# One slab forward in a seven-product FFN chunk: order of a down slab, a later block load and an accumulator bank

## The chip, the cores and the metric

The kernel runs on one core of one Trainium2 chip, in one launch. The metric is the device time of the launch in microseconds (us).

## The reference

Two layers over 256 tokens of 1024 values (fp32). Each layer has a SwiGLU FFN, a mixer (convolution, linear recurrence and pooling side by side), a cross attention over 256 memory rows, and a second SwiGLU FFN, each with a residual and a layer norm. The change lies in the FFNs alone:

```python
def swiglu(x, w_gate, w_up, w_down):          # x 256x1024, d_ff = 2816
    return (jax.nn.silu(x @ w_gate) * (x @ w_up)) @ w_down

for l in range(2):
    h = layer_norm(ALPHA * h + 0.5 * swiglu(h, ffn1_gate[l], ffn1_up[l], ffn1_down[l]), ...)
    # mixer, cross attention
    h = layer_norm(ALPHA * h + 0.5 * swiglu(h, ffn2_gate[l], ffn2_up[l], ffn2_down[l]), ...)
```

## The kernel before

**Arithmetic.** fp32 values are kept as two parts, a high and a low one: `split` (L61, L62) has ScalarE cast the source to the high part and VectorE subtract that from the source to give the low part. A product then takes three matmuls (high x high, low x high, high x low; `mm_rows` and L112), which all accumulate in one PSUM bank. Weights come in raw tiles of 128x1024 (512 KB), and each is split into a `whi` and a `wlo` tile. These two pools have 8 buffers each, so a new split waits until TensorE is done with the part 8 back.

**An FFN.** `ffn()` goes through the hidden width in chunks of 512 columns (the last has 256). For a chunk it forms gate and up products for the 256 tokens (two halves of 128), applies SiLU and the multiplication, and `turn` brings the result to the layout that the down projection needs (four DMAs at L455, two transposes on VectorE, a split into `ah` and `al`). The down projection is cut in slabs: `both(c, u)` loads half of chunk `c`'s rows of `down`, splits it and issues 24 matmuls into four banks named `dn`, which are held open through the whole FFN. Slabs run one or two chunks behind the hidden chunks.

**The seven-product chunk.** Chunks in `sevens` don't form the eight block products (2 token halves x gate and up x 2 halves of the 1024 inputs) but seven, in the manner of Strassen, with sums of weight blocks and of blocks of x (`bx`, prepared once per FFN). There are two such chunks in the first FFN and three in each of the other three: 11 in all. The function is `by_seven`. Its four weight blocks are `w00` and `w10` (gate, upper and lower inputs) and `w01` and `w11` (up), two raw tiles each. Their homes rotate from chunk to chunk over three pairs of buffers (`spare0/1`, `lng/lnb` and two of the six `raw`).

`parts_of(r, plus)` adds a second block to the first in place on VectorE (L606), if there is one, and splits it. `run(o, x, w)` issues a product's 12 matmuls of 128x512. `taken` copies a bank to SBUF on ScalarE (L635), `put` combines a bank with SBUF on VectorE (L625), and `more` adds a block's other half of inputs to a raw tile by an accumulating DMA from GpSimd's queue (L643). Each chunk takes banks from the pool `acc`, which has 4, as `dn` has.

In program order before the change, a chunk does on TensorE:

| step | product | into | behind it |
| --- | --- | --- | --- |
| 1 | x00 x `w00` | `o[0]` | `taken` to `s` |
| 2 | bx0 x (`w00+w01`) | `o[1]` | `more(w01)` |
| 3 | x01 x `w10` | `o[2]` | |
| 4 | bx1 x (`w00+w01+w11`) | `o[0]`, added | `more(w00)`, `put(s)`, `taken(e)` |
| 5 | first slab, `between[0]` = `both(c-2, 1)` | `dn` | SiLU of `s` |
| 6 | bx2 x `w01` (with the accumulated half) | `o[0]`, added | `taken(f)` |
| 7 | second slab, `between[1]` = `both(c-1, 0)` | `dn` | `put(f)` from `o[1]` |
| 8 | bx3 x `w11` | `o[1]`, added | |
| 9 | x11 x `w00` (with the accumulated half) | `o[0]`, added | `left()`: SiLU, `put(e)` from `o[1]`, mult, `turn` |

The sum of `w11` onto `w00+w01` in step 4 is called the second sum below.

**What sets the order.** The kernel is written in program order, and a scheduler then orders the instructions of each engine by its own costs. It need not keep the order above: in the kernel before, it put matmuls of the first slab ahead of or among those of step 4 in some chunks. Each engine then runs its queue strictly in order, as do the DMA queues of SP (all loads and `turn`'s four DMAs) and of GpSimd (`more`).

Of the kernel before, what the change touches and what calls it, by code (L numbers as in the profile page):

```python
# [12 lines left out]
ALU = mybir.AluOpType  # L13
# [4 lines left out]
P = 128  # L18
# [10 lines left out]
CHUNK = 512  # L29
# [17 lines left out]
def model(ctx: ExitStack, tc: tile.TileContext, t: dict, out: bass.AP):  # L47
# [6 lines left out]
    def acc(shape=(P, 2, SEQ), tag="acc"):  # L54
        return ps.tile(list(shape), F32, tag=tag, name=tag)
# [4 lines left out]
    def split(hi, lo, src):  # L60
        nc.scalar.copy(hi, src)  # L61
        lows.append(nc.vector.tensor_tensor(lo, src, hi.bitcast(F32), op=ALU.subtract))  # L62
# [73 lines left out]
    def mm_rows(o, xh, xl, wh, wl, start, stop, more=False):  # L136
        product(o, xh, wh, start, False, more)
        product(o, xh, wl, False, False, more)
        product(o, xl, wh, False, stop, more)

    def tok(i):
        return slice(i * P, (i + 1) * P)
# [264 lines left out]
    def ffn(l, name, n, pend=None, last=False, early=None):  # L407
        gate, up, down = (t[f"{name}_{x}"][l] for x in ("gate", "up", "down"))
        with tc.tile_pool(name="ffn", bufs=2, reuse_waits="tile") as fp:
# [19 lines left out]
            def activations():  # L429
                return fp.tile([P, NT, CHUNK], F32, tag="sg", name="sg", bufs=1)  # L430
# [3 lines left out]
            def ordered(v):  # L434
                return v.rearrange("p (a k j) -> p a k j", a=4, j=32)

            def in_order(o):
                return o.rearrange("p (a j k) -> p a k j", a=4, j=32)

            def activate(s, i, og):  # L440
                nc.scalar.activation(ordered(s[:, i, :]), in_order(og), AF.Silu)
# [9 lines left out]
            def turn(s):  # L451
                ah, al = act_tiles()
                x = fp.tile([P, 4, NT, P], F32, tag="dealt", name="dealt", bufs=1)
                for a in range(4):
                    nc.sync.dma_start(x[a * 32 : a * 32 + 32], s[:, :, a * P : (a + 1) * P])  # L455
                d = fp.tile([P, NT, 4, P], F32, tag="up", name="square", bufs=1)
                for i in range(NT):
                    nc.vector.transpose(  # L458
                        d[:, i].rearrange("p k (b r) -> p b k r", b=4),
                        x[:, :, i, :].rearrange("p b (k j) -> p b k j", k=4),  # L460
                    )
                d = d.rearrange("p i k t -> p k i t")
                split(*(y.rearrange("p k (i t) -> p k i t", i=NT) for y in (ah, al)), d)
                return ah, al
# [110 lines left out]
            def by_seven(c0, bx, between):  # L575
                def rows_by_columns(r):
                    return r.rearrange("p (k c) -> p k c", c=CHUNK)

                def pieces(*tags):
                    return [  # L580
                        rows_by_columns(
                            (fp if "spare" in g else wp).tile([P, DM], F32, tag=g, name="raw", bufs=6 if g == "raw" else 1)
                        )
                        for g in tags
                    ]

                def block(m, j, to):
                    for i in range(2):
                        k = 4 * j + 2 * i
                        loads.append(nc.sync.dma_start(  # L590
                            to[i], m[k * P : (k + 2) * P, c0 : c0 + CHUNK].rearrange("(k p) c -> p k c", p=P)
                        ))
                    return to

                homes = [("spare0", "spare1"), ("lng", "lnb"), ("raw", "raw")]
                n = sevens.index(c0 // CHUNK)
                w00 = block(gate, 0, pieces(*homes[n % 3]))
                w01 = block(up, 0, pieces(*homes[(n + 1) % 3]))
                w10 = block(gate, 1, pieces("spare2", "raw"))
                w11 = block(up, 1, pieces(*homes[(n + 2) % 3]))  # L600

                def parts_of(r, plus=None):
                    hi, lo = [], []
                    for i in range(2):
                        if plus is not None:
                            nc.vector.tensor_tensor(r[i], r[i], plus[i], op=ALU.add)  # L606
                        h = wp.tile([P, 1024], F32R, tag="whi", name="whi", bufs=8)
                        w = wp.tile([P, 1024], F32R, tag="wlo", name="wlo", bufs=8)
                        h, w = (rows_by_columns(x) for x in (h, w))
                        split(h, w, r[i])  # L610
                        hi.append(h)
                        lo.append(w)
                    return Weights(hi, lo, 2, [])

                def part_of_x(i, j):
                    d = slice(4 * j, 4 * j + 4)
                    return xTh[:, d, tok(i)], xTl[:, d, tok(i)]

                def run(o, x, w, more=False):
                    for k in range(4):  # L620
                        wh, wl = w.at(k, slice(0, CHUNK))
                        mm_rows(o, x[0][:, k, :], x[1][:, k, :], wh, wl, k == 0 and not more, k == 3, more)

                def put(o, a, op, b):
                    nc.vector.tensor_tensor(ordered(o), in_order(a), ordered(b), op=op)  # L625

                s = activations()  # L630
                ef = fp.tile([P, NT, CHUNK], F32, tag="up", name="halves", bufs=1)
                e, f = ef[:, 0, :], ef[:, 1, :]

                def taken(o, bank):
                    nc.scalar.copy(ordered(o), in_order(bank))  # L635

                o = [acc((P, CHUNK)) for _ in range(3)]
                run(o[0], part_of_x(0, 0), parts_of(w00))
                taken(s[:, 0, :], o[0])
                def more(to, m, j):  # L640
                    for i in range(2):
                        k = 4 * j + 2 * i
                        nc.gpsimd.dma_start(  # L643
                            to[i], m[k * P : (k + 2) * P, c0 : c0 + CHUNK].rearrange("(k p) c -> p k c", p=P),
                            accum_op=ALU.add,
                        )

                run(o[1], bx[0], parts_of(w00, w01))
                more(w01, up, 1)
                run(o[2], part_of_x(0, 1), parts_of(w10))  # L650
                run(o[0], bx[1], parts_of(w00, w11), True)
                more(w00, gate, 1)
                put(s[:, 0, :], o[2], ALU.add, s[:, 0, :])
                taken(e, o[0])
                between[0]()
                nc.scalar.activation(s[:, 0, :], s[:, 0, :], AF.Silu)
                run(o[0], bx[2], parts_of(w01), True)
                taken(f, o[0])
                between[1]()
                put(f, o[1], ALU.subtract, f)  # L660
                run(o[1], bx[3], parts_of(w11), True)
                run(o[0], part_of_x(1, 1), parts_of(w00), True)


                def left():
                    activate(s, 1, o[0])
                    put(e, o[1], ALU.subtract, e)
                    nc.vector.tensor_tensor(s, s, ef, op=ALU.mult)  # L668
                    return turn(s)

                return left
# [27 lines left out]
            bx = []  # L699
# [541 lines left out]
```

## Time and profile before

| what | before |
| --- | --- |
| three timed runs | 1079.6, 1079.92 and 1082.12 us; median 1079.92 us |
| profiled execution | 1078.62 us, of it 1076.9 us span |
| mean granted TensorE clock | 0.999 |
| bytes read from HBM | 239.22 MB, 223 GB/s over the span |
| instructions | 16377 |

In the views that follow, PE is TensorE's matmuls and PEld its weight loads, DVE is VectorE, ACT ScalarE, POOL GpSimd and SP the engine that issues the loads. A row of a timeline has a start, a duration (both in us), the engine, the line of the kernel, the operation with `out<-in`, the shapes, a count of instructions that were put together, and in brackets how long the engine sat idle before it and whose work ended that. A row of the waits has the waiting engine and tile, what it waited for, then the total in us, the number of times and the longest. In a chain's row stand the start, the length and the work. Matmuls are pipelined, so a matmul's own duration (0.38 us) is longer than the distance between two starts.

The seven-product chunks lie at about 76 to 136 us (first FFN), 420 to 512 us, 589 to 681 us and 949 to 1041 us.

### The profile page before, as it was taken

The numbers are of one execution on the slowest core, as the hardware profiler recorded it, in microseconds if no ns is written. First come the engines' busy times: TensorE is split into PE (matmuls) and PEld (weight loads), VectorE is DVE, ScalarE is ACT, GpSimd is POOL, SyncE is SP. The second block draws the span as 40 slices with busy tenths as digits, with TensorE's granted clock in tenths as the row PEclk, the third lists the DMA queues.
The fourth block names the chain that finished last, engine by engine and source line by source line (L and its number), as shares of the span: only waits on it lengthen the run. The fifth ranks groups of instructions, "written<-read, shape, count | busy, mean of one in ns | idle before, by whom it ended". The sixth has DMA issues, their size and how long they took to land.

```text
span 1076.9 us, 16377 instructions
## 1 busy us (share of the span) xinstructions
PE 1056.5 (98%) x5918; PEld 925.8 (86%) x5918; DVE 947.1 (88%) x1257; ACT 671.2 (62%) x920; POOL 119.0 (11%) x158
## 2 busy tenths in 40 slices
PE   9999999999999999999999999999999999999997
PEld 7888788989889888888888888888898998888886
DVE  6979987998998799999798999888989788999986
ACT  7548665757467566668475767566764665666661
POOL 9701101000000001110001011010000000001100
PEclk9999999999999999999999999999999999999999
DMA  9999993764475589999679999857536665899981
GB/s 366 263 296 252 252 324 133 251 196 161 173 263 174 179 269 255 285 270 289 225 269 260 278 300 225 315 175 230 189 128 213 240 228 177 274 286 259 225 283 41
DMA packets 142864, 254.98 MB, mean 237 GB/s; under 512 B 10112, under 2 KB 49312, under 8 KB 142784
## 3 DMA queue, kind: packets, MB, share of 16 engines
q1 hardware_dynamic: 129024, 228.49, 63.2%
q0 software_dynamic: 13184, 24.27, 13.2%
q10 hardware_dynamic: 576, 1.18, 0.3%
q8 instruction: 46, 0.75, 0.3%
q14 instruction: 34, 0.28, 0.1%
HBM read 239.22 MB, written 1.05 MB: 223 GB/s over the span
## 4 chain that ended last, share of the span: by engine, by line
PE 69%; DVE 14%; DMA 6%; issue 6%; ACT 5%; SPq 1%; DVEq 0%; ACTq 0%
PE acc L112 47%; PE dn L112 20%; DVE wlo L62 6%; ACT whi L61 4%; DMA dealt<-sg 2%; DVE raw L606 2%; DMA raw<-in_ffn_gate_dram 1%; DMA raw<-in_ffn_up_dram 1%; PE acc L179 1%; SPq L455 1%; DVE square L458 1%; DMA raw<-in_ffn_down_dram 1%; DVE sg L668 1%; PE dn L943 1%; ACT ah L61 0%
## 5 line engine op out<-in xcount | busy, mean ns | idle before, releaser
L61 ACT CAST whi<-raw 128x1024 fp32r<-128x1024 f32 (+1 forms) x462 | 465.8, 1041 | 202.2 <-PE dn L112 58.9
L62 DVE TENSOR_TENSOR wlo<-raw,whi 128x1024 fp32r<-128x1024 f32 (+1 forms) x462 | 544.0, 1208 | 51.1 <-ACT whi L61 42.4
L112 PE MATMUL acc<-whi,xT 128*128 128x512 f32 x872 | 266.5, 380 | 0.0
L112 PEld LDWEIGHTS acc<-whi,xT 128*128 128x128 f32 x872 | 164.8, 189 | 23.3
L112 PE MATMUL acc<-wlo,xT 128*128 128x512 f32 x436 | 165.2, 379 | 0.0
L112 PE MATMUL acc<-xT,whi 128*128 128x512 f32 x576 | 142.2, 382 | 0.4 <-DVE xT L62 0.3
L112 PE MATMUL dn<-wlo,ah 128*128 128x512 f32 x346 | 132.2, 382 | 2.6 <-DVE wlo L62 2.6
L112 PE MATMUL dn<-whi,ah 128*128 128x512 f32 x346 | 129.9, 382 | 4.5 <-ACT whi L61 3.3
L112 PE MATMUL dn<-whi,al 128*128 128x512 f32 x346 | 130.3, 380 | 0.3
L112 PEld LDWEIGHTS acc<-xT,whi 128*128 128x128 f32 x576 | 103.9, 190 | 12.7 <-ACT whi L61 0.9
L112 PEld LDWEIGHTS acc<-wlo,xT 128*128 128x128 f32 x436 | 82.4, 189 | 11.5
L112 PE MATMUL dn<-whi,xT 128*128 128x512 f32 x288 | 87.9, 381 | 0.0
L112 PEld LDWEIGHTS dn<-whi,ah 128*128 128x128 f32 x346 | 65.2, 189 | 16.4 <-ACT whi L61 4.9
L112 PEld LDWEIGHTS acc<-xT,wlo 128*128 128x128 f32 x576 | 75.5, 191 | 3.9
L112 PEld LDWEIGHTS dn<-wlo,ah 128*128 128x128 f32 x346 | 65.4, 189 | 14.8 <-DVE wlo L62 6.0
L112 PE MATMUL acc<-xT,wlo 128*128 128x256 f32 x576 | 75.9, 275 | 0.0
L112 PEld LDWEIGHTS dn<-whi,al 128*128 128x128 f32 x346 | 65.1, 189 | 11.3 <-DVE al L62 2.3
L112 PE MATMUL acc<-whi,kTh 128*128 128x512 f32 x176 | 67.5, 384 | 3.4 <-ACT halves L635 1.8
L112 PE MATMUL acc<-wlo,kTh 128*128 128x512 f32 x176 | 66.7, 379 | 0.0
L112 PE MATMUL acc<-whi,kTl 128*128 128x512 f32 x176 | 66.7, 379 | 0.0
L357 POOL TENSOR_TENSOR rs<-rs,nhalf 128x1 f32<-128x1 f32 x16 | 14.9, 933 | 434.0 <-DVE rs L353 307.1
L112 PEld LDWEIGHTS dn<-whi,xT 128*128 128x128 f32 x288 | 54.4, 189 | 7.7 <-DVE xT L62 0.3
(236 smaller groups left out, 1357.8 us busy)
## 6 DMA issues: line engine op xcount, KB each, us to landing
raw<-in_ffn_up_dram SPq DMA_DIRECT2D x88, 512.0 KB, 5.7
raw<-in_ffn_down_dram SPq DMA_DIRECT2D x88, 512.0 KB, 6.4
raw<-in_ffn_gate_dram SPq DMA_DIRECT2D x84, 512.0 KB, 5.9
raw<-in_w_in_dram SPq DMA_DIRECT2D x48, 512.0 KB, 4.8
raw<-in_ffn_up_dram POOLq DMA_DIRECT2D x22, 512.0 KB, 6.0
raw<-in_ffn_gate_dram POOLq DMA_DIRECT2D x22, 512.0 KB, 7.9
dealt<-sg SPq DMA_DIRECT2D x80, 128.0 KB, 4.3
raw<-in_ca_k_dram SPq DMA_DIRECT2D x16, 512.0 KB, 5.1
```

Of the source, the lines that this page charges most:

```text
L61: nc.scalar.copy(hi, src)
L62: lows.append(nc.vector.tensor_tensor(lo, src, hi.bitcast(F32), op=ALU.subtract))
L112: nc.tensor.matmul(o, w, x, start=start, stop=stop, skip_group_check=more)
L179: nc.tensor.transpose(pt[:, k, :], src[:, (4 * j + k) * P : (4 * j + k + 1) * P], unit)
L357: nc.gpsimd.tensor_tensor(rs, rs, nhalf[:, 0:1], op=ALU.pow)
L455: nc.sync.dma_start(x[a * 32 : a * 32 + 32], s[:, :, a * P : (a + 1) * P])
L458: nc.vector.transpose(d[:, i].rearrange("p k (b r) -> p b k r", b=4), x[:, :, i, :].rearrange("p b (k j) -> p b k j", k=4),)
L606: nc.vector.tensor_tensor(r[i], r[i], plus[i], op=ALU.add)
L668: nc.vector.tensor_tensor(s, s, ef, op=ALU.mult)
L943: nc.tensor.matmul(o[g, hh, :], kc[:, hh, g], x, start=True, stop=True)
```

## The change

In a seven-product chunk the first slab moves from behind step 4 to in front of it, and `put(s)` with it. `w11` is loaded after that slab (program order), no longer with the other three blocks. The second slab moves from behind bx2 to in front of it. bx3's product gets a fourth bank, `o[3]`, and no longer accumulates on `o[1]`. `e` is therefore formed in two steps: `o[1]` is taken early, and `o[3]` is added in `left()`, one VectorE instruction more in each chunk. Matmuls and DMAs are the same in number and size.

```diff
                 w10 = block(gate, 1, pieces("spare2", "raw"))
-                w11 = block(up, 1, pieces(*homes[(n + 2) % 3]))
...
+                o = [acc((P, CHUNK)) for _ in range(3)]
+                run(o[0], part_of_x(0, 0), parts_of(w00))
+                taken(s[:, 0, :], o[0])
                 run(o[1], bx[0], parts_of(w00, w01))
                 more(w01, up, 1)
                 run(o[2], part_of_x(0, 1), parts_of(w10))
+                between[0]()
+                put(s[:, 0, :], o[2], ALU.add, s[:, 0, :])
+                w11 = block(up, 1, pieces(*homes[(n + 2) % 3]))
                 run(o[0], bx[1], parts_of(w00, w11), True)
                 more(w00, gate, 1)
-                put(s[:, 0, :], o[2], ALU.add, s[:, 0, :])
                 taken(e, o[0])
-                between[0]()
+                between[1]()
                 nc.scalar.activation(s[:, 0, :], s[:, 0, :], AF.Silu)
+                put(e, o[1], ALU.subtract, e)
                 run(o[0], bx[2], parts_of(w01), True)
                 taken(f, o[0])
-                between[1]()
+                o.append(acc((P, CHUNK)))
+                run(o[3], bx[3], parts_of(w11))
                 put(f, o[1], ALU.subtract, f)
-                run(o[1], bx[3], parts_of(w11), True)
                 run(o[0], part_of_x(1, 1), parts_of(w00), True)
 
                 def left():
                     activate(s, 1, o[0])
-                    put(e, o[1], ALU.subtract, e)
+                    put(e, o[3], ALU.add, e)
                     nc.vector.tensor_tensor(s, s, ef, op=ALU.mult)
                     return turn(s)
```

The three lines with a plus at `o = [acc(...)` stood a little higher before, ahead of the definition of `more`; they are not new.

More of the change, by code (lines that the diff above doesn't have):

```diff
@@ L635, in taken @@
                     nc.scalar.copy(ordered(o), in_order(bank))
-                o = [acc((P, CHUNK)) for _ in range(3)]
-                run(o[0], part_of_x(0, 0), parts_of(w00))
-                taken(s[:, 0, :], o[0])
                 def more(to, m, j):
```

## Prediction

> **What bounds the kernel now.** I read the page's first two parts, then the chain of waits, then what TensorE waits for, then the timelines around the block-product chunks.
>
> ```profile
> span 1076.9 us, 16377 instructions
> PE 1056.5 (98%) x5918; PEld 925.8 (86%) x5918; DVE 947.1 (88%) x1257; ACT 671.2 (62%) x920; POOL 119.0 (11%) x158
> PEclk9999999999999999999999999999999999999999
> ```
> ```profile
> 380.76 33.67 PE acc L112 x156
> ```
>
> TensorE is busy 98% of the span at a full clock. The second fence is a piece of the chain: 156 matmuls of 128x512 in 33.67 us, 0.2158 us from start to start. The change keeps every matmul, so only time in which that beat is broken can be won. The next view lists what TensorE itself (not its weight loads) waited for, over the whole kernel.
>
> ```profile
> PE dn L112 <- ACT whi L61: 3.3, 4, 0.9
> PE dn L112 <- DVE wlo L62: 2.6, 7, 1.0
> PE acc L112 <- ACT halves L635: 1.8, 2, 1.6
> PE acc L112 <- ACT sg L635: 1.6, 4, 0.8
> ```
> ```profile
> 123.53 0.38 PE L112 MATMUL acc<-whi,xT 128*128 128x512 f32 x1
> 124.77 0.48 PE L112 MATMUL dn<-whi,ah 128*128 128x512 f32 x1 [0.87 <-ACT whi L61]
> ```
>
> These four groups are 9.3 us, and they lie in the chunks that the change touches. A gap costs more than its idle column: from 123.53 to 124.77 is 1.24 us, 1.02 over the beat, for 0.87 idle, thus 0.15 more for each of the 17. That makes about 12 us, 1.1% of the span, and it bounds any gain from above.
>
> What makes these gaps is VectorE, which has almost as much to do there as TensorE. The first row here is a window over most of a second chunk of the FFN at 420 to 530 us, with busy time of PE, PEld, DVE, ACT and POOL, clock and DMA share; the second covers the third.
>
> ```profile
> 453.00:482.00 29.00, 28.02 (x128) 23.59 (x127) 27.69 (x27) 20.97 (x24) 3.90 (x4) 1.00 1.01 269
> 482.00:512.00 30.00, 28.89 (x137) 24.59 (x136) 27.90 (x28) 22.09 (x25) 2.38 (x2) 1.00 0.94 279
> ```
>
> **A ledger of VectorE's lead.** A chunk is 7 products of 12 matmuls and two slabs of 24, 132 in all, or 132 x 0.2158 = 28.5 us of TensorE. VectorE's turn of the second chunk goes from its first split, at the end of the first row here, to the same split one chunk on.
>
> ```profile
> 434.97 3.82 DVE L62 TENSOR_TENSOR wlo<-raw,whi 128x1024 fp32r<-128x1024 f32 x3 [0.65 <-ACT whi L61]
> 453.89 6.90 DVE L62 TENSOR_TENSOR wlo<-raw,whi 128x1024 fp32r<-128x1024 f32 x6 [1.17 <-ACT whi L61]
> 469.78 1.22 DVE L62 TENSOR_TENSOR wlo<-raw,whi 128x1024 fp32r<-128x1024 f32 x1 [0.39 <-ACT whi L61]
> 470.92 0.68 DVE L625 TENSOR_TENSOR halves<-acc,halves 128x512 f32<-128x512 f32 x1
> 471.52 1.21 DVE L606 TENSOR_TENSOR raw<-raw 128x1024 f32<-128x1024 f32 x1
> ```
> ```profile
> 445.35 0.38 PE L112 MATMUL acc<-whi,xT 128*128 128x512 f32 x1
> 456.30 0.48 PE L112 MATMUL dn<-wlo,ah 128*128 128x512 f32 x1 [0.22 <-DVE wlo L62]
> 460.56 0.48 PE L112 MATMUL acc<-whi,kTh 128*128 128x512 f32 x1 [0.76 <-ACT sg L635]
> ```
>
> The third split of the first row starts at about 437.5, so the turn is 469.78 - 437.5 = 32.3 us, 3.8 more than TensorE's. TensorE begins the last product (`x11`) of the chunk before at 445.35 and the second chunk 12 matmuls later, at 447.94: VectorE is 10.4 us ahead there. A split takes 1.15 us from start to start (6.90 for six), a `put` 0.60 (470.92 to 471.52), a sum or a mult, of a split's size, 1.15 too.
>
> The lead needed is set by the first down slab. Its first low part is the second split of the row at 453.89, over at 456.2. TensorE wants it at its second slab matmul, and in this chunk the planner had put slab matmuls right behind `w10`: 447.94 + 37 x 0.2158 = 455.9. The lead needed is 10.4 plus the 0.22 us of the idle column: it is just missed. The second wait, 0.76 us, is `taken(s)` standing in ScalarE's queue behind seven casts.
>
> **The change, part by part.**
>
> *Slab ahead of the second sum.* The slab's splits now come ahead of the splits of the second sum (`w00+w11`) in VectorE's order. In the second chunk 13 of its instructions remain from the first split to the slab's first low part: 7 splits, 3 sums (the scheduler leaves one half of the second sum in front), 2 puts, 1 mult, so 11 x 1.15 + 2 x 0.60 = 13.9 us. VectorE also waits in its alternation with ScalarE, 1.2 us (the 1.17 above) to 2. TensorE takes 37 x 0.2158 = 7.98 us to that matmul. Lead needed: 7.1 to 7.9 us. In the third chunk both halves of that sum are behind, 12.7 us of work: 5.9 to 6.75, and I take 6.75, because the one ScalarE wait that shows is 1.17 and the changed order has a `put` more that can wait.
>
> *One more put a chunk.* `put(e, o[3], ADD, e)` is new: 11 of them, 0.60 us each by the start-to-start above, 0.68 by the whole row.
>
> ```profile
> L625 DVE TENSOR_TENSOR halves<-acc,halves x22: 678/682/684, 108.6 to 1035.0; 128x512 f32<-128x512 f32 x22
> who waited for it (us, times):
>   ACT whi L61: 0.5, 1
> ```
>
> VectorE's turn goes from 32.3 to 32.9, or stays at 32.4 where its wait of 1.17 shortens. If TensorE followed VectorE at every step, 11 x 0.68 = 7.5 us would be the price; with the lead as cover, nothing. The ledger below carries it.
>
> *The lead at the start of a chunk becomes smaller.* The pools of `whi` and `wlo` have 8 buffers, so the cast of the next chunk's first block half goes when TensorE is done with the part 8 back.
>
> ```profile
> 436.48 1.05 ACT L61 CAST whi<-raw 128x1024 fp32r<-128x1024 f32 x1 [0.24 <-PE acc L112]
> 452.81 6.73 ACT L61 CAST whi<-raw 128x1024 fp32r<-128x1024 f32 x7 [4.08 <-DVE raw L606]
> 459.92 0.59 ACT L635 COPY sg<-acc 128x512 f32<-128x512 f32 x1 [0.38 <-ACT whi L61]
> ```
>
> In the first row that cast is let go by TensorE at 436.48: 8 back is the first half of `bx[2]`'s block, which stands before the second slab. In the new order 8 back is the first half of the second slab, now before `bx[2]`: released 42 matmuls, 9.07 us, before the next chunk, where the release at 436.48 was 11.46 before 447.94. The lead becomes 10.4 - 2.4 = 8.0 us.
>
> *The three later FFNs.* Second chunk: a lead of 8.0 against a need of 7.1 to 7.9, no loss. Third chunk: the lead is less by a turn's deficit, 32.4 to 32.9 against 28.5, so 3.6 to 4.1, I take 4.0; needed 6.75; a gap of 2.75 and 0.15, thus 2.9 us. The wait behind the seven casts goes, since `taken(s)` stands behind fewer. Before, the waits of these three FFNs were 9.3 less the first FFN's 4.0 (below), in 12 gaps: 5.3 + 12 x 0.15 = 7.1 us. After, 3 x 2.9 = 8.7: the change costs +1.6. With the need at 5.9 and the lead at 4.1 it is 3 x 1.95 = 5.9, a gain of 1.2; with the lead at 3.6 and a miss in the second chunk of as much as its idle column before (0.22), 3 x 3.7, a loss of 4.
>
> *The first FFN* (chunks at 76 to 136 us) has only two such chunks, so no third that pays the debt.
>
> ```profile
> PE dn L112 <- DVE wlo L62: 1.0, 1, 1.0
> PE dn L112 <- ACT whi L61: 0.9, 1, 0.9
> PE acc L112 <- ACT sg L635: 0.3, 1, 0.3
> ```
> ```profile
> 122.73 1.99 ACT L61 CAST whi<-raw 128x1024 fp32r<-128x1024 f32 x2 [5.40 <-DVE raw L606]
> ```
>
> These three are TensorE's waits from 76 to 136 us beside the `halves` group above, which lies wholly here (1.6 and 0.2): 4.0 us idle. The slab's first cast stands 5.40 us behind the second sum (122.73); with the slab ahead of it the two `dn` waits go, 1.9 + 2 x 0.15 = 2.2 us. The short `sg` and `halves` waits, 0.3 + 0.2 + 2 x 0.15 = 0.8, I count as gone too, as with fewer casts in front of those copies. The long one, 1.6, is `bx[2]` waiting for `taken(e)`. In the new order that copy stands behind a cast which waits for the gate accumulate (7.8 us to land, below), so I leave it. Gain 3.0 us; 4.75 if the copy is in time, 0.6 if its wait doubles and the short ones stay.
>
> *The fourth block's load behind the slab.* SP now issues `w11`'s two loads after the slab's.
>
> ```profile
> 464.87 5.08 SPq L590 DMA_DIRECT2D raw<-in_ffn_up_dram  x4
> ```
> ```profile
> raw<-in_ffn_up_dram SPq DMA_DIRECT2D x4, 512.0 KB, 4.9
> raw<-in_ffn_down_dram SPq DMA_DIRECT2D x3, 512.0 KB, 7.8
> raw<-in_ffn_gate_dram POOLq DMA_DIRECT2D x2, 512.0 KB, 7.8
> ```
>
> These are issues and median us to landing in the second chunk. `w11` is wanted a slab later too, so I count its move at nothing. What it must not meet is the third chunk's `w01`: its home is the second chunk's `w11`, free from the first split of `bx[3]`'s block, and the sum that reads it follows six VectorE instructions later (five splits, a put): 5 x 1.15 + 0.60 = 6.35 us. Before, the issue at 464.87 and the sum at 471.52 left 6.65. At 4.9 us it is in time. [...]
>
> *A bank for `bx[3]`.* The product no longer waits until `put(f)` has read `o[1]`. But nothing waited: in the rows on L625 its only waiter is a cast, 0.5 us. Nothing is won, and nothing lost while a fourth `acc` bank is free, since the next chunk's first product takes one that was read long before. The Trainium skill (PSUM — Partial Sum Buffer, "PSUM bank collisions raise a hardware error") says that two engines must never touch one bank's quadrant together, so an own bank should take a wait off TensorE; the sum by it would be lower by that wait, which the trace does not have.
>
> **Sum.** -3.0 + 1.6 = -1.4 us. The profiled run took 1078.62 (span 1076.9 and 1.72 around it), so 1077.2 for such a run. The three timed runs have a median of 1079.92, 1.3 above; I predict 1079.92 - 1.4 = 1078.5. About 0.3%, 3.2 us, is what can be told from no change.
>
> **Rivals.**
>
> *A, all waits go.* The slab in front gives so much slack that the ring of 8 doesn't matter: -12, 1068. For it: the waits behind the second sum are the largest. Against: VectorE's turn stays over TensorE's by 4 us. Half way, -6: 1074, if the third chunk's need is met because VectorE's 1.2 to 2 us of waits shrink and `taken(e)` comes in time. Chance of over 3.2 us gained: 0.32.
>
> *B, VectorE's work shows at the end.* The put, 0.68 us, is paid in both the second and third chunk of three FFNs (4.1 us) on top of the sum: +2.7, 1082.6. For it: 27.69 us busy in a window of 29. Against it: the third chunk's gap lets VectorE catch up. It lies within the forecast's range.
>
> *C, slower: `w01` comes late.* Third chunk only, three FFNs; each us of landing over 6.35 delays VectorE's sum, and so the slab, one for one. To be slower by 3.2 it takes (3.2 + 1.4)/3 = 1.55 over, a landing of 7.9.
>
> ```profile
> 53.08 9.91 DMA dealt<-sg
> 1031.69 7.97 DMA raw<-in_ffn_down_dram
> ```
>
> Such landings exist in the chain. At 9.0, between the two, it costs 3 x 2.65 = 8: +6.6, 1086.5. Against it: two loads instead of four are issued there, and up loads took 4.9. The copy of `e` with its wait doubled and the leads at their worst (+3.4) end there too; this side gets 0.22.
>
> *D, nothing moves.* The planner orders the engines, but the new order does hold in every chunk, so only the sizes can cancel; this is inside the forecast.
>
> **How the numbers follow.** Forecast, with B and D (within 3.2 us of before) 0.46, A with its half-way form 0.32, C and what ends with it 0.22. The range leaves out the full A and the far end of C: it goes from -7.5 (1072.5), a little past half of A, to +4.6 (1084.5), a landing of about 8.35.
>
> **What would show it.** Right: no TensorE wait on `dn` at 124.8; in each later FFN waits of 2 to 3 us in front of the third chunk's first slab, and none over 0.3 in the second; casts of the next chunk released by a `dn` matmul, not `acc`; VectorE's turn 32.4 to 32.9. Wrong: DVE idle on `raw<-in_ffn_up_dram` in front of a sum (C); no wait at all in the third chunk (A); a wait on `halves` over 1.7 us at about 103 (worst case of the first FFN).

## The result and the profile after

The changed kernel takes 1077.32 us (median of 20 runs, 1075.17 to 1080.84), the kernel before 1079.7 us (median of 20 runs beside them): a ratio of 0.9982 with a 95% interval of 0.9974 to 0.9989, which is 1.2 to 2.8 us. The forecast was 1.4 us less and within 0.3% of no change. The profiled execution of the changed kernel is one of its longest runs, 1080.84 us. A second execution of the same order was therefore profiled (`a1_again` below, 1076.26 us).

The page after, its span and busy times:

```profile
span 1079.1 us, 16365 instructions
PE 1057.2 (98%) x5918; PEld 927.9 (86%) x5918; DVE 953.9 (88%) x1268; ACT 670.1 (62%) x920; POOL 118.6 (11%) x158
```

What TensorE waited for after the change (total, times, longest), to be read beside the 9.3 us of before:

```profile
PE acc L112 <- ACT halves L634: 5.5, 2, 5.2
PE acc L112 <- DVE wlo L62: 2.0, 3, 0.7
PE dn L112 <- DVE al L62: 1.8, 3, 0.6
...
PE acc L112 <- ACT sg L634: 1.3, 3, 0.4
```

The `dn` waits on `whi` and `wlo` have left the list. A single wait of 5.2 us has come in, in the first FFN; in the second execution the same row is shorter:

```profile
PE acc L112 <- ACT halves L634: 3.4, 1, 3.4
```

Four stretches of the trace say where time went. Each begins and ends at the start of the same TensorE instruction in every trace (the last one at the last matmul):

| stretch (times of before) | before | before again | changed | changed again |
| --- | --- | --- | --- | --- |
| first FFN from its first seven-product chunk, 75.05 to 177.45 | 102.40 | 101.42 | 103.45 | 101.80 |
| second FFN and norm, 414.27 to 537.52 | 123.25 | 123.26 | 123.55 | 122.23 |
| third FFN and norm, 583.30 to 706.13 | 122.83 | 123.54 | 123.20 | 122.51 |
| last FFN, 943.11 to 1069.29 | 126.18 | 126.14 | 125.70 | 125.51 |

The last FFN is the cleanest: 0.4 to 0.7 us less, and 125.5 in all five experiments below that leave the three later FFNs as changed (a2, a3, a4, b2, c2). Over those five and the two traces of the table, the three later FFNs take 371.1 us in the mean, against 372.6 in the two traces of before: 1.5 us less, where single traces of one order differ by up to 2.2. The first FFN comes out the same within its own scatter of 2 us.

### The profile page after: what moved, and what is told of

It reads as the page before. It is cut to its first block, busy times and chain, and to the rows that moved or that the text cites. A ratio compares the mean times of both kernels' runs of the same rounds, so it can differ in the third digit from the quotient of the medians.

```text
span 1079.1 us, 16365 instructions
## 1 busy us (share of the span) xinstructions
PE 1057.2 (98%) x5918; PEld 927.9 (86%) x5918; DVE 953.9 (88%) x1268; ACT 670.1 (62%) x920; POOL 118.6 (11%) x158
## 3 DMA queue, kind: packets, MB, share of 16 engines
HBM read 239.22 MB, written 1.05 MB: 223 GB/s over the span
## 4 chain that ended last, share of the span: by engine, by line
PE 69%; DVE 15%; DMA 7%; issue 5%; ACT 4%; SPq 1%; DVEq 0%; ACTq 0%
PE acc L112 47%; PE dn L112 19%; DVE wlo L62 8%; DMA raw<-in_ffn_up_dram 2%; ACT whi L61 2%; DMA raw<-in_ffn_gate_dram 2%; DMA dealt<-sg 2%; DVE raw L605 1%; PE acc L179 1%; DVE square L458 1%; DVE al L62 1%; ACT ah L61 1%; DMA raw<-in_ca_k_dram 1%; DVE halves L624 1%; DMA raw<-in_ffn_down_dram 1%
```

## The experiments

All kernels are written with one switch for each part of the change, so that parts can be undone singly; `early` is set in the first FFN alone. The diffs are shortened to what a switch does. Each ratio is to the kernel before, on the same chip.

**a1, the change once more.** No edit.

> The changed kernel once more, with its by_seven written with four switches (all on); the order on every engine is the same. The profiled run of the changed kernel had one wait of 5.15 us in front of TensorE's x11 product at 117 us (first FFN), behind the copy of f. Theory 1 (that wait hangs on when the next chunk's w00 lands, and so differs from run to run): another profile shows this wait with another length, between 0 and 6 us, the three later FFNs keep 2.4 us of waits each within 0.3, and the times spread over about 5 us with a median near 1077.3. Theory 2 (it is a fixed consequence of the new order): the wait is 5.2 us again within 0.5.

Measured: 1077.33 us, ratio 0.9984 (0.997 to 0.9998), runs from 1076.02 to 1082.43. The wait was 3.4 us, so it differs from run to run (theory 1), and the later FFNs' waits in these chunks are those of the first profile, but for one of 0.3 us. Their place is the third chunk. The first three rows are TensorE's waits there, the last two the windows of the second and third chunk (busy PE, PEld, DVE, ACT, POOL, clock, DMA share), cut at the same times as those of before:

```profile
482.53 0.48 PE L112 MATMUL acc<-wlo,xT 128*128 128x512 f32 x1 [0.67 <-DVE wlo L62]
490.79 0.48 PE L112 MATMUL acc<-whi,kTh 128*128 128x512 f32 x1 [0.44 <-ACT sg L634]
494.67 0.48 PE L112 MATMUL dn<-whi,al 128*128 128x512 f32 x1 [0.59 <-DVE al L62]
```
```profile
453.00:482.00 29.00, 28.81 (x132) 24.29 (x130) 27.78 (x28) 18.79 (x22) 4.78 (x4) 1.00 0.99 284
482.00:512.00 30.00, 28.44 (x135) 24.33 (x136) 29.06 (x29) 21.38 (x26) 2.42 (x2) 1.00 0.99 279
```

The second chunk waits for nothing; the third waits 1.70 us in three places, 2.2 over the beat. VectorE is busy 29.06 of 30 us in the second window, where it was 27.90 before.

**a2, the old order in the first FFN alone.**

```diff
-    all four parts on
+    all four parts off if early is not None else all four parts on
```

> The old order of the four steps in the first FFN, the new order in the three later FFNs. Theory 1 (all of the change in time, gain and spread, is in the first FFN; the later three cost the same in both orders, 7.5 us before and 7.7 after): about 1079.7, no different from before within 0.7 us, and a spread of 3 us or less as before had. The prediction's ledger (first FFN gains 3.0, later ones lose 1.6): 1081.3. Rival (the gain comes from the later FFNs): 1077.3.

Measured: 1078.23 us, ratio 0.9989 (0.9977 to 1.0001). That is 1.2 us less than before (-0.1 to 2.5), some two thirds of the 1.7 that a1 kept, with only the later FFNs changed. It speaks against the ledger's 1081.3, and rather against theory 1, which had no gain here; it agrees with the 1.5 us of the stretches. Its runs spread over 5.6 us, where theory 1 had 3 or less. The times alone settle neither that there is a gain (the interval reaches past 1) nor whether the first FFN adds to it: the two ratios overlap.

**a3, the second slab back behind bx2 in the first FFN.** The wait of up to 5.2 us is `x11`, into `o[0]`, waiting until the copy of `f` has been read from it. Here is ScalarE's queue in front of that copy, and SP's issue of the second chunk's `w00` (the rows of two gate loads at 103.08), in the changed kernel:

```profile
105.91 0.58 ACT L634 COPY halves<-acc 128x512 f32<-128x512 f32 x1
109.61 1.05 ACT L61 CAST whi<-raw 128x1024 fp32r<-128x1024 f32 x1 [3.12 <-DMA raw<-in_ffn_gate_dram]
112.25 1.04 ACT L61 CAST whi<-raw 128x1024 fp32r<-128x1024 f32 x1 [1.59 <-DMA raw<-in_ffn_gate_dram]
113.53 1.04 ACT L61 CAST whi<-raw 128x1024 fp32r<-128x1024 f32 x1 [0.24 <-DMA raw<-in_ffn_gate_dram]
115.92 1.04 ACT L61 CAST whi<-raw 128x1024 fp32r<-128x1024 f32 x1 [1.35 <-DVE raw L605]
116.87 0.58 ACT L634 COPY halves<-acc 128x512 f32<-128x512 f32 x1
```
```profile
103.08 1.65 SPq L590 DMA_DIRECT2D raw<-in_ffn_gate_dram  x2
```

and the same issue in the kernel before, where it goes out with a third load of the gate:

```profile
98.35 3.37 SPq L590 DMA_DIRECT2D raw<-in_ffn_gate_dram  x3
```

The copy of `e` (105.91) is in time. The copy of `f` (116.87) stands behind four casts: one waits for the accumulated half of `w00`, two for the next chunk's `w00`, which was issued 4.7 us later than before, and one for a sum on it. The load is late because its home is `w01`'s, and that is read by bx2's splits, now behind the second slab's.

```diff
+    if early is None: between[1]()
     run(o[0], bx[2], parts_of(w01), True)
     taken(f, o[0])
+    if early is not None: between[1]()
```

> As changed, but in the first FFN alone the second slab stands behind bx2 again, so that the splits of w01 for bx2, which free the home of the next chunk's w00, come before the slab's. Theory 1 (the late w00 load makes the copy of f late): w00 of the second chunk is issued some 4 us earlier (before: 98.35, changed: 103.08), the wait of up to 5.15 us at 117 goes, the time is 1074 to 1076 with the narrow spread of before. Rival (the load is late because SP's queue carries w11 later): the wait stays, time 1077 to 1078.

Measured: 1080.03 us, ratio 1.0009 (0.9997 to 1.0022). The load is issued at 97.55, as theory 1 had it, and the wait for `f` is gone. But others have come, and the time is no better, where theory 1 had 1074 to 1076:

```profile
PE acc L112 <- ACT halves L634: 3.1, 3, 1.6
PE dn L112 <- DVE al L62: 2.4, 4, 0.6
PE dn L112 <- ACT ah L61: 2.1, 4, 1.0
```

The first row is now mostly bx2 waiting for the copy of `e` (1.05 and 1.63 us in the first FFN): with the second slab gone from between bx1 and bx2, both of which go into `o[0]`, nothing covers that copy. So the run does not show what an earlier load alone would bring.

**a4, `w11` loaded with the other blocks.** The order of every engine but SP stays.

```diff
+    w11 = block(up, 1, ...)          # behind w10
...
-    w11 = block(up, 1, ...)          # behind the first slab
```

> As changed, but w11 is loaded with the other three blocks, as before the change; only SP's order differs. Theory 1: the wait in front of x11 in the first FFN stays, as its load waits for the home and not for SP; 1077.3 within 1 us. Rival (w11's late load collides with the next chunk's w00 on the DMA engines): the wait falls to under 1.5 us and the time to 1075 or less. If SP's queue is instead held up by w11's wait for its home, loads behind it are late in all FFNs: over 1079.

Measured: 1077.19 us, ratio 0.9983 (0.997 to 0.9995): the same as the change (theory 1). Where `w11`'s load stands costs nothing and brings nothing. The wait for `f` was 2.0 us in its profile, the shortest of the three, but the times don't differ.

**b1, the kernel before once more.** No edit.

> The kernel before once more, with its by_seven written with four switches (all off); the order on every engine is the same. It gives a second profile of it. Theory 1 (its waits are fixed by the order, and only the long wait of the first FFN for the copy of e, 1.56 us in the first profile, moves from run to run): the dn waits at 124 us again 0.87 and 0.96, the later FFNs again 2.4 to 3.1 us each over the beat, median 1079.8. Rival (before loses more than its one profile showed): the later FFNs lose 3.5 us or more in this one.

Measured: 1079.55 us, ratio 0.9998 (0.9986 to 1.0011), theory 1. Its trace is the column "before again": the `dn` waits of the first FFN are again 0.87 and 0.97, the wait for `e` is 0.73 instead of 1.56, and the later FFNs lose 2.9 to 3.1 us each over the beat in their three chunks (2.5 to 2.9 in the first profile). This counts every gap of over 0.12 us from start to start, less the beat; by the same count a1 loses 2.4 to 2.5, of which 2.2 in the three places of the third chunk.

**b2, the copy of `f` ahead of the next chunk's casts, first FFN.**

```diff
+    with tc.issue_after(copy_of_f.ins):      # of the chunk before
+        p00 = parts_of(w00)
```

> As changed, but in the first FFN ScalarE's copy of f is ordered ahead of the casts of the second chunk's w00 (it stood behind them, and they wait for loads that land at 109 to 113 us). Theory 1 (TensorE's wait of 2.0 to 5.2 us in front of x11 is this place in the queue): the wait on halves goes or falls under 1 us; a part comes back as a wait of the second chunk's first product for its own casts, 0 to 2 us; 1074 to 1076.5. Rival (the loads are late for everything, so the wait only moves): 1077 to 1078 with waits of the same sum on whi or wlo in the second chunk's first product.

Measured: 1081.55 us, ratio 1.0013 (1.0001 to 1.0025). The rival was right that the wait only moves, and the time is even longer than it said. TensorE's waits in the first FFN are now these:

```profile
118.80 0.48 PE L112 MATMUL acc<-whi,xT 128*128 128x512 f32 x1 [1.17 <-ACT whi L61]
130.19 0.48 PE L112 MATMUL acc<-wlo,kTh 128*128 128x512 f32 x1 [0.76 <-DVE wlo L62]
146.40 0.48 PE L112 MATMUL acc<-whi,xT 128*128 128x512 f32 x1 [3.04 <-ACT halves L634]
```

The last is the same wait one chunk later: the second chunk's copy of `f` behind four casts, of which the first waited 4.09 us for a transfer of the gate.

```profile
141.99 3.88 ACT L61 CAST whi<-raw 128x1024 fp32r<-128x1024 f32 x4 [4.09 <-DMA raw<-in_ffn_gate_dram]
145.78 0.57 ACT L634 COPY halves<-acc 128x512 f32<-128x512 f32 x1
```

**b3, the first slab alone.** Of the change only `between[0]` and `put(s)` in front of the second sum.

```diff
+    between[0]()
+    put(s[:, 0, :], o[2], ALU.add, s[:, 0, :])
     run(o[0], bx[1], parts_of(w00, w11), True)
...
-    between[0]()
     run(o[0], bx[2], parts_of(w01), True)
```

> Of the change only the first slab (with put(s)) in front of the second sum; the second slab, w11's load and bx3's bank as before. The prediction's ledger: the lead at the start of a chunk stays 10.4 us as 8 parts back is again bx2's block, while the need falls to 7.9 and 6.75, so the later FFNs' waits (7.1 to 7.5 us) and the dn waits of the first FFN (2.2) nearly all go: 1070.5 to 1073. Rival (the lead is set by more than the ring, so the third chunk still waits 2 us or more): 1076 to 1078. If the copy of e becomes late in more chunks: 1079 or over.

Measured: 1093.59 us, ratio 1.0125 (1.0105 to 1.0144). The ledger's 1070.5 to 1073 is far off; it is the expectation's last case, the copy of `e` late in more chunks. Waits of TensorE, the row for the copies, and one of its eight places with ScalarE's queue there:

```profile
PE acc L112 <- ACT halves L634: 17.1, 8, 4.0
```
```profile
475.14 0.80 PE L112 MATMUL acc<-whi,kTh 128*128 128x512 f32 x1 [2.55 <-ACT halves L634]
```
```profile
473.55 1.04 ACT L61 CAST whi<-raw 128x1024 fp32r<-128x1024 f32 x1 [3.09 <-DMA raw<-in_ffn_gate_dram]
474.50 0.58 ACT L634 COPY halves<-acc 128x512 f32<-128x512 f32 x1
```

It is a3's finding on a larger scale: the slab that moves forward was the cover of the copy of `e` between bx1 and bx2, and the casts in front of the copy wait for loads. In the full change the second slab takes its place.

**b4, the bank alone.** Of the change only `o[3]` and the put that it adds.

```diff
-    run(o[1], bx[3], parts_of(w11), True)
+    o.append(acc((P, CHUNK)))
+    run(o[3], bx[3], parts_of(w11))
...
-    put(e, o[1], ALU.subtract, e)
+    put(e, o[3], ALU.add, e)                 # o[1] taken earlier by a put of its own
```

> Of the change only bx3's own bank, with the put that it adds in each chunk; the order of steps is as before. The prediction's step (nothing waited for that bank, and the put is covered by the lead or costs its 0.6 us in a chunk that waits): 1079.8 to 1082, waits of the later FFNs longer by 0 to 1.2 us each. Rival (the bank frees a wait): under 1079.

Measured: 1079.43 us, ratio 1.0002 (0.9992 to 1.0011), between the two expectations. In the old order the bank and its 11 puts together change nothing; the run does not part the two.

**c1, everything but the bank.** The reverse of b4's diff, in the new order.

> As changed, but bx3 accumulates on o[1] as before, after put(f) has read it. Theory 1 (the bank is free of worth in the old order, where the second slab stood between the copy of f and bx3, but in the new order bx2 and bx3 touch): TensorE waits at bx3 for the copy of f and put(f), 0.58 + 0.68 and their hand-overs, up to 2 us in each of 11 chunks, less what the scheduler fills with the next chunk's products: 1083 to 1095. The prediction's step (nothing is won by that bank): within 1 us of the changed kernel, 1077 to 1078.

Measured: 1095.8 us, ratio 1.0149 (1.0136 to 1.0162), theory 1. The way is not quite as expected: the scheduler filled the place with the next chunk's products, so little waits on `put(f)` itself, and the loss shows at other copies:

```profile
PE acc L112 <- ACT sg L634: 9.5, 7, 1.6
PE acc L112 <- ACT halves L634: 4.8, 8, 1.0
PE acc L112 <- ACT whi L61: 2.9, 1, 2.9
PE acc L112 <- DVE halves L624: 1.9, 5, 0.5
```

**c2, less to load in the first FFN.** The accumulate of the gate block is left out in its two chunks, so that `w00` keeps only its sum there.

```diff
-    more(w00, gate, 1)
+    if early is None: more(w00, gate, 1)
```

> As changed, but the first FFN's two chunks leave out the accumulate of the gate block's other half (4 transfers of 512 KB on GpSimd's queue), so w00 keeps only its sum there; all other instructions and their order are the same. Theory 1 (the first FFN's wait for the copy of f is set by when loads land, and the DMA engines are full there): the wait of 2.0 to 5.2 us falls under 1 us, w00's loads land 1.5 us or more earlier, 1073.5 to 1075.5. Rival (the wait is the queue's order alone): the wait stays over 2 us, 1077 to 1078.

Measured: 1074.48 us, ratio 0.9953 (0.994 to 0.9966), theory 1. The median landing time of SP's gate loads from 90 to 115 us, first in the changed kernel and then here (6.4 us in the kernel before):

```profile
raw<-in_ffn_gate_dram SPq DMA_DIRECT2D x3, 512.0 KB, 9.1
```
```profile
raw<-in_ffn_gate_dram SPq DMA_DIRECT2D x3, 512.0 KB, 4.8
```
```profile
PE dn L112 <- DVE al L62: 0.6, 1, 0.6
```

The last row, of the kernel with less to load, is all that TensorE waits for from 75 to 140 us. The first FFN's stretch takes 99.8 us and the runs lie within 1.3 us. The edit also takes away one cast's wait for the accumulate itself, so it shows that the transfers set this wait, not how much each of them does.

**c3, 7 buffers of `whi` and `wlo`.** `bufs=8` becomes `bufs=7` in both places of both pools.

> As changed, with 7 buffers of whi and of wlo instead of 8. The prediction's step on the lead (it is set by the part 8 back): with 7 the release comes 12 slab matmuls, 2.6 us, later, so the second chunk waits 2 us where it waited none and the third 2 to 4.6 us more; over three FFNs 12 to 20 us: 1089 to 1097. Rival (the lead is set by VectorE's own work or by the loads): under 1081.

Measured: 1080.99 us, ratio 1.0012 (1.0001 to 1.0022), so the rival, if only just, and far from the 1089 to 1097 of the step on the lead. TensorE's waits on low parts come more often, most of them short:

```profile
PE acc L112 <- DVE wlo L62: 6.8, 15, 1.8
```

The three later FFNs take 370.3 us in this trace, as in a1 (370.3): there a ring of 7 costs no time, though the waits stand in other places. What 7 cost lies in the rest of the kernel: outside the four stretches it takes 605.9 us of the span, against 602.2 to 604.1 in the other traces.

**c4, one put less.** `put(e, o[1], ...)` is left out, so bx0's product is missing from `e`; VectorE has 11 instructions less.

> As changed, but put(e, o[1]) is left out (the product with bx0 is missing from e); VectorE has 11 instructions less, ScalarE's, SP's and GpSimd's order is the same. The prediction's ledger (each put in the second and third chunk of a later FFN takes 0.6 us from the lead that the third chunk lacks): the third chunk's waits fall from 2.0 us idle to about 0.8 in each of three FFNs, 1073 to 1074.5. Rival (those waits stand on the ring and on turn's split of al, not on the put): 1076.5 to 1078.

Measured: 1076.49 us, ratio 0.9969 (0.9959 to 0.9979). The third chunk's waits in the second FFN, to be read beside a1's 0.67, 0.44 and 0.59:

```profile
483.56 0.48 PE L112 MATMUL acc<-wlo,xT 128*128 128x512 f32 x1 [0.25 <-DVE wlo L62]
491.82 0.48 PE L112 MATMUL acc<-whi,kTh 128*128 128x512 f32 x1 [0.44 <-ACT sg L634]
495.70 0.48 PE L112 MATMUL dn<-whi,al 128*128 128x512 f32 x1 [0.59 <-DVE al L62]
```

Only the first gives way, by 0.42 us here (0.45 and 0.20 in the next two FFNs): mostly the rival. The put costs the later FFNs about 1 us in all.

None of these, with the whole computation in it, is clearly faster than the change; a4 is its equal.

## Why the prediction was right, and where not

The total was right (-1.4 forecast; 1.2 to 2.8 less measured), and so was its frame: all that can be won is some 12 us of waits, and the change trades some for others. But the total was right by luck. Its two terms were both wrong, by about 3 us each and with opposite signs.

*The three later FFNs, +1.6 forecast, about -1.5 measured.* That the debt is paid in the third chunk and the second waits for nothing was right. So was the lead, in its size too. In a1's trace the cast of the second chunk's first block half waits 2.30 us for a `dn` matmul, the part 8 back, as forecast, and VectorE's first split waits for that cast. The last two rows are the starts of `x11`; the next chunk begins 12 matmuls later.

```profile
438.53 1.05 ACT L61 CAST whi<-raw 128x1024 fp32r<-128x1024 f32 x1 [2.30 <-PE dn L112]
439.61 1.23 DVE L62 TENSOR_TENSOR wlo<-raw,whi 128x1024 fp32r<-128x1024 f32 x1 [2.12 <-ACT whi L61]
467.45 6.89 DVE L62 TENSOR_TENSOR wlo<-raw,whi 128x1024 fp32r<-128x1024 f32 x6
481.25 4.63 DVE L62 TENSOR_TENSOR wlo<-raw,whi 128x1024 fp32r<-128x1024 f32 x4
444.81 0.38 PE L112 MATMUL acc<-whi,xT 128*128 128x512 f32 x1
473.67 0.38 PE L112 MATMUL acc<-whi,xT 128*128 128x512 f32 x1
```

TensorE begins the second chunk at 447.4, 7.8 us behind the split at 439.61 (8.0 forecast). It begins the third at 476.26, 4.2 us behind that chunk's first split, the fifth of the row at 467.45, at 472.0 (4.0 forecast). VectorE's turn between these two splits is 32.4 us, as forecast.

The step that failed is the need of 6.75, with 1.2 to 2 us of ScalarE alternation charged to VectorE. From 472.0 to the first slab's first low part, the third split of the row at 481.25, VectorE takes the 12.7 us of work that the prediction counted and waits for nothing. The need there is 4.7. A larger one stands earlier, where the prediction did not look: the first low part of `w10` is over at 482.45, 10.4 us behind the first split, and TensorE wants it 25 matmuls, or 5.4 us, into the chunk. That is a need of 5.0 against the lead of 4.2, and the gap of 0.8 is the first wait of the third chunk. The other two are `taken(s)` and the `al` of `turn`. Together they come to 2.2 us over the beat, not 2.9. The 7.1 us put down for before was also too small, since it left the shortest gaps out: by the count under b1 the three FFNs lose 7.9 and 9.0 us in the two traces of before and 7.4 in a1. The waits thus make 0.5 to 1.6 us of the gain, and the 1.5 of the stretches lies within that.

What did not follow from the lead is the price of a smaller ring: with 7 buffers (c3) these FFNs take as long as with 8. Nor does a put cost them what the ledger said: its share is 0.2 to 0.45 us an FFN (c4), a third or less of the 1.2 us that the ledger gave two puts, which also answers *rival B*.

*The first FFN, -3.0 forecast, 0 within 2 us measured.* The `dn` waits (2.2) and the short copies (0.8) went as forecast. The long wait did not stay at 1.6: it went from the copy of `e` to the copy of `f`, and is 2.0, 3.4 or 5.2 us in three profiles of the new order, with 1.6 us more at a low clock behind the longer two (last section). The step that failed here is leaving that wait at 1.6: the prediction looked at the cast in front of the copy of `e` and missed that moving the second slab delays bx2's splits, hence the home of the next `w00`, hence a load at a time when the transfers take 9.1 us. It gave that move no price but the ring. c2 shows that the transfers set the wait. The copy's earlier place does not get the time back (b2), nor does the load's earlier issue where it is had by moving the second slab back (a3).

*The bank.* That nothing waited and nothing is won holds for the old order (b4). In the new order it is the condition for moving the second slab: without it, and with `e` formed in one step again, the change costs 16 us instead of bringing 2 (c1). The reason in the prediction was taken from the trace of before, where the slab still stood between `put(f)` and bx3. The Trainium skill's rule on a bank shared by two engines (PSUM — Partial Sum Buffer, "PSUM bank collisions raise a hardware error") pointed the right way, and the trace of c1 agrees with it: 1.9 us of waits are on `put(f)` directly. That the waits at other copies follow from the same bank is argued from the order, not shown by a run of its own.

*`w11`'s load* at nothing was right (a4). *Rival C* did not happen: VectorE has no idle time on an up load in the third chunk. *Rival A* did not either.

## What to carry to other kernels

A block of matmuls between two products into the same bank is the cover of the copy that reads the bank in between: before moving it, name what covers that copy afterwards. Parts of such a change can't be priced one at a time from the trace of before (the first slab alone +14 us, all but the bank +16, all together -2): each part is priced in the order that the others leave. A moved step moves its splits, and they decide when a home is free for the next load, so follow each buffer that it reads to the load behind it.

## What the runs showed of the hardware

Long waits of TensorE cost more than their length. In these traces each of the ten that lasted 2.12 to 5.15 us was followed by a low clock. Windows in the changed kernel around its wait of 5.15 us, then in a4 behind its wait of 1.95 us (the clock is the column ahead of the DMA share):

```profile
112.00:117.00 5.00, 0.35 (x2) 0.00 (x0) 3.59 (x4) 3.17 (x4) 0.89 (x1) 1.00 0.85 336
117.00:121.00 4.00, 3.50 (x9) 2.84 (x10) 4.00 (x5) 1.41 (x3) 1.03 (x2) 0.57 0.79 130
```
```profile
114.00:118.00 4.00, 4.00 (x20) 3.49 (x20) 4.00 (x6) 1.94 (x3) 1.20 (x1) 1.00 0.84 132
```

After the long wait the granted clock is 0.57 over four us, some 1.6 us more lost. The same low clock followed waits of 3.36 us (a1, 0.57) and of 2.12 and 2.55 us (b3, 0.57 and 0.58); behind 1.95 us the clock stayed at 1.00. So in the three profiles of the new order the wait for `f` costs either 2 us or, with its tail, 5 to 7. That fits the changed kernel's wider scatter, as c2's runs without the wait lie within 1.3 us. The Trainium skill (TensorE: Matmul & The Clock Gate, "What's actually happening") gives about 3.4 us of idleness for the clock to fall; here 2.12 us were enough.

The length of one wait does not decide it alone. In a2 the clock fell behind two short waits, of 0.87 us at 124.14 and 0.96 us at 125.58, while behind the same two waits it stayed at 1.00 in both traces of before:

```profile
126.00:130.00 4.00, 4.00 (x13) 3.20 (x12) 4.00 (x5) 3.30 (x4) 0.00 (x0) 0.57 1.07 192
```

What set it there stays open.
